# A written-out order of instructions in place of a planner, in a one-core hybrid SSM and attention block

## The chip, the cores and the metric

The kernel runs on one core of a Trainium2 chip. The time is the device time of one execution in microseconds (us). Five engines of the core take part, each with its own stream of instructions, which it runs in the order in which it finds them: PE (TensorE, the matrix multiplications and the transposes), DVE (VectorE), ACT (ScalarE), POOL (GpSimd) and SP (SyncE, which here only issues DMA transfers). An instruction waits on semaphores for the work of other engines, and everything behind it on its own engine waits with it. Nothing about what is computed changes in this case; only the order on each engine does.

## The reference

One layer of a hybrid block over 2048 positions of width 1024 in float32:

```python
hn = rmsnorm(h, mix_norm_g[i])
proj = hn @ w_in[i]
u, g_ssm, q, k, v, g_attn = jnp.split(proj, SPLITS, axis=-1)      # 512 columns each
y_ssm = s5_branch(u, ...) * jax.nn.silu(g_ssm)
y_att = stick_breaking_branch(q, k, v, q_g, k_g) * jax.nn.silu(g_attn)
h = h + jnp.concatenate([y_ssm, y_att], axis=-1) @ w_out[i]
ple_gate = jax.nn.sigmoid(rmsnorm(h, ple_norm_g[i]) @ w_ple_gate[i])
h = h + ple_gate * (p[i] @ w_ple_proj[i])
```

`s5_branch` is a diagonal complex state space model of 32 groups of 16 channels with 64 states each, followed by GELU and a gated linear unit (a 512 x 1024 matrix). `stick_breaking_branch` is causal attention with 8 heads of 64: with z = qk/8, a key's weight is sigmoid(z) times the product of sigmoid(-z) over all later keys before the query, so a block of queries walks through its keys from the latest to the earliest with a running product.

## The kernel before

Positions are handled in 16 tiles of 128. Matrix products of float32 data are made of three passes over a high and a low part of each operand (the three calls at L541 to L543, and L707 to L709). The stages, with the times in the profiled execution:

- **Start** (0 to some 130 us, `phase_u`): x is loaded and normalised (ACT squares and sums at L596, DVE scales the sum, POOL takes the power -1/2 at L507 into `rs_x`, ACT scales x at L598), PE transposes it (`ps_x`, L526), and the first 512 columns of the projection come out as `ps_u` (L541 to L543). The first two tiles are read already transposed (`x_189`, `x_190`, L561); their own sums go over POOL additions (L577) and `rs0`, `rs1` (L581). DVE meanwhile works through a chain of some 300 small operations for the state space tables.
- **State space** (to some 315 us): 8 batches, with the gate's products (`ps_sg`) between them.
- **Attention** (to some 1085 us): 4 pairs of heads, each a pass over the 16 tiles, the passes overlapping. `attn_proj` makes q, k, v and gate of a tile: PE adds up `ps_q` (L745) in two banks, ACT and DVE bring it out (L751, L65), ACT and DVE form the sums of squares (L762, L764, L72), POOL takes the power (`rs_qk`, L507), DVE scales (`qn`, L65), PE transposes (`ps_tq`, L526). v is shifted by one position through two SP transfers (L753, L755) and subtracted on POOL (L756). `attn_block` makes, for each chunk of up to 512 keys, `ps_z` (PE, L812, in two banks, one for each head), `px` (ACT sigmoid L816; POOL mask L819 in the chunk on the diagonal; DVE scan L821), the transposes `ps_wt` (PE, L526), `ws` (two ACT evictions, L835) and `ps_o` (PE, L843).
- **Gated linear unit** (some 860 to 1085 us), among the last attention steps: `ps_v` and `ps_g` (L541 to L543) and their gating on ACT, DVE and POOL (L696, L76, L698), and sums of weight blocks for the last stage (`cross_sums`: SP loads L868, POOL L874 to L877, SP stores L879).
- **Output** (1085 us to the end): `mixed_pair` (products with W_out, `ps_h`) and `gated_pair` (transposes `ps_t`, gate products `ps_g`, `ps_p`, and the stores).

PE works in three modes in this kernel: on all of the array; on halves of the rows (`ps_q`, `ps_z`, `ps_wt`, `ps_tq`: two instructions side by side, `64*128` in the profile); and on halves of the columns (`ps_o`, `128*64`). The transposes `ps_wt` and `ps_tq` all go to one pair of PSUM banks (`e.pair`), so each group of them must wait until the `ws` (or q, k, g) evictions of the group ahead have emptied it. `ps_z` of a chunk must wait in the same way for the scans of the chunk that had its banks.

What sets the order: the program is emitted as one list, tile after tile. Then `plan` works out from addresses which instruction needs which, and `duration` gives each a length by a formula (an SP transfer costs SP 0.45 us whatever it is); `list_schedule` plays the program engine by engine, taking on each the ready instruction of the best rank, with a penalty of 0.09 us for a change of the PE mode and a preference of 4 us for staying in it; `best_order` repeats this forwards and backwards six times and keeps the shortest; `arrange` then ties each instruction to the one ahead of it on its engine. In that model an instruction on PE may start as soon as one that it needs on PE has started, and on the other engines when it is done, with no time in between.

Of the kernel before, what the change touches and what calls it, by code (L numbers as in the profile page):

```python
# [18 lines left out]
P = 128  # L19
# [4 lines left out]
G = 32  # L24
GH = 16
ST = 64
# [1255 lines left out]
def footprint(ap, offset, shape):  # L1282

    row = 1
    for n in shape[1:]:
        row *= n
    p0, m = offset // row, 1
    f = offset % row + sum((n - 1) * s for s, n in ap[1:] if s < 0)
    for s, n in ap[1:]:
        if s and n > 1:  # L1290
            m = sum(m << (abs(s) * k) for k in range(n)) if n * abs(s) > 64 or m != 1 or s not in (1, -1) else (1 << n) - 1
    return p0, p0 + ap[0][1], m << f


def duration(i, name, outs, ins, psum):

    n = max([a[1] for a in outs + ins] or [1])
    eng = str(i.engine).split(".")[-1]
    if name == "InstDMACopy":
        names = [a.bass_ap.tensor.name for a in i.ins if getattr(a, "bass_ap", None) is not None]  # L1300
        return (0.6 if eng == "Pool" else 0.45), (4.0 if any("ssm_w_glu" in k for k in names) else 0.0)
    if name == "InstMatmult":
        cols, kind = outs[0][1], ins[0][2]
        if i.is_transpose:
            return (0.031 if ins[0][0] <= 64 else 0.109), 0.11
        if "float32r" in kind or "bfloat16" in kind:
            return max(cols / 2400.0 + 0.0136, 0.107) / (2 if ins[0][0] <= 64 else 1), 0.11
        half = min(outs[0][0], ins[0][0]) <= 64
        return (0.5 if outs[0][0] <= 32 else 1 if half else 2) * max(cols / 1160.0, 0.056), 0.12
    if eng == "Activation":  # L1310
        return (0.05 if psum else 0.094) + n * 0.00083, 0.065 if psum else 0.03
    if eng == "Pool":
        if name == "InstTensorTensor" and "pow" in str(i.op).lower():
            return 0.35 + 0.15 * n, 0.08
        base, slope = {"InstMemset": (0.04, 0.0008), "InstTensorCopy": (0.4, 0.001), "InstTensorScalarPtr": (0.25, 0.001), "InstTensorScalarAffineSelect": (0.14, 0.0008)}.get(name, (0.12, 0.00186))
        return base + slope * n, 0.09
    if name == "InstTensorScalarPtr" and i.is_tensor_tensor_scan:
        return 0.05 + n * 0.0022, 0.03
    if name in ("InstMemset", "InstTensorCopy", "InstTensorScalarPtr") and not psum and not i_tt(i):
        return 0.07 + n * 0.0006, 0.03  # L1320
    return 0.07 + n * 0.00104, 0.03


def i_tt(i):

    return getattr(i, "is_scalar_tensor_tensor", False)


def plan(tc, pools):

    mybir_i = list(tc.nc.cur_bb.bb.instructions)
    first, last = 16512, 229344
    open_l, open_r, open_b, base, slots, spans, over, home, used = [], [], [], {}, {}, [], {}, {}, {}
    for p in sorted(pools, key=lambda p: p.id):
        kb = int(p.kb_per_partition_size() * 1024)
        sp = str(p.space).split(".")[-1]
        if sp == "DRAM":
            base[p.id] = 0
        else:
            side = open_b if sp == "PSUM" else open_r if "right" in str(p.side) else open_l  # L1340
            born = int(p.alloc_inst.name.split("-")[1])
            while side and side[-1][2] is not None and side[-1][2] < born:
                side.pop()
            at = side[-1][0] if side else 0 if side is open_b else last if side is open_r else first
            lo = at - kb if side is open_r else at
            end = p.release_inst
            side.append((lo if side is open_r else lo + kb, p.id, None if end is None else int(end.name.split("-")[1])))
            base[p.id] = lo
            for q, l2, h2, e2, s2 in spans:
                if sp == s2 and l2 < lo + kb and lo < h2 and e2 is not None and int(e2.name.split("-")[1]) < int(p.alloc_inst.name.split("-")[1]):  # L1350
                    over.setdefault(p.alloc_inst.name, []).append(e2.name)
            spans.append((p.id, lo, lo + kb, end, sp))
        for sp, size, tag, addr, _ in p.gen_slots(0):
            home[tag] = p.alloc_inst.name, p.release_inst.name if p.release_inst is not None else None
            slots.setdefault(tag, []).append((str(sp).split(".")[-1], base[p.id] + addr, size // P))
    turn, tiles, held, pre, length, opened, soft, mode = {}, {}, {}, [], [], {}, [], {}
    number = {i.name: k for k, i in enumerate(mybir_i)}
    for k, i in enumerate(mybir_i):
        if type(i).__name__ == "BassTilePoolBoundary":
# [5 lines left out]
        for w, accs in ((0, i.ins), (1, i.outs)):  # L1365
            for a in accs:
                b = getattr(a, "bass_ap", None)
                if b is None:
                    continue
                t, n = b.tensor, 1  # L1370
                ap = [(int(s), int(c)) for s, c in b.ap]
                for s, c in a.ap[1:]:
                    n *= int(c)
# [249 lines left out]
```

## Time and profile before

| | |
|---|---|
| median of 3 runs | 1476.32 us (1475.82 to 1478.0) |
| profiled execution | 1474.24 us, of which the profile's span is 1472.5 us |
| mean granted TensorE clock | 0.994 |
| PE busy | 1436.7 us (98%) |
| DVE, ACT, POOL busy | 1009.0 (69%), 810.4 (55%), 474.8 us (32%) |
| DMA | 238.21 MB, 162 GB/s on average |

The span is the time between the first and the last record of the engines. The busy time of PE is that in which at least one matrix instruction is under way; weight loads (PEld) run beside it. PE's idle time is therefore 1472.5 - 1436.7 = 35.8 us, and the time that PE spends on changes of mode, or at a lower clock, is part of its busy time.

### The profile page before, as it was taken

The numbers are of one execution on the slowest core, as the hardware profiler recorded it, in microseconds if no ns is written. First come the engines' busy times: TensorE is split into PE (matmuls) and PEld (weight loads), VectorE is DVE, ScalarE is ACT, GpSimd is POOL, SyncE is SP. The second block draws the span as 40 slices with busy tenths as digits, with TensorE's granted clock in tenths as the row PEclk, the third lists the DMA queues.
The fourth block names the chain that finished last, engine by engine and source line by source line (L and its number), as shares of the span: only waits on it lengthen the run. The fifth ranks groups of instructions, "written<-read, shape, count | busy, mean of one in ns | idle before, by whom it ended". The sixth has DMA issues, their size and how long they took to land.

```text
span 1472.5 us, 33586 instructions
## 1 busy us (share of the span) xinstructions
PE 1436.7 (98%) x13068; PEld 1224.2 (83%) x13068; DVE 1009.0 (69%) x1817; ACT 810.4 (55%) x1765; POOL 474.8 (32%) x512
## 2 busy tenths in 40 slices
PE   6999999999999999999999999999999999999998
PEld 5999889988888888888888877777778888778786
DVE  8953977977567786678766775666778557754444
ACT  5654555565555766567655665555665345533432
POOL 3131363522221211221121124443334554534432
PEclk8999999999999999999999999999999999999999
DMA  8886845645333433334332455766568556523221
GB/s 289 288 287 205 250 143 186 206 143 168 128 130 125 144 112 114 114 130 140 121 126 102 142 146 171 226 218 178 155 201 280 176 171 200 166 65 101 93 72 58
DMA packets 179054, 238.21 MB, mean 162 GB/s; under 512 B 65760, under 2 KB 121296, under 8 KB 167760
## 3 DMA queue, kind: packets, MB, share of 16 engines
q1 hardware_dynamic: 176512, 227.49, 48.0%
q0 software_dynamic: 2384, 8.59, 2.0%
q8 instruction: 103, 1.69, 0.5%
q14 instruction: 55, 0.45, 0.1%
HBM read 166.94 MB, written 64.90 MB: 157 GB/s over the span
## 4 chain that ended last, share of the span: by engine, by line
PE 81%; DVE 7%; DMA 3%; ACT 3%; issue 3%; POOL 2%; SPq 1%; POOLq 0%; DVEq 0%; ACTq 0%
PE ps_q L745 21%; PE ps_o L843 7%; PE ps_z L812 6%; PE ps_wt L526 4%; PE ps_g L707 4%; PE ps_h L709 4%; PE ps_h L707 3%; PE ps_h L708 3%; PE ps_g L709 3%; PE ps_g L708 3%; DMA v<-qn 2%; PE ps_u L541 1%; PE ps_u L543 1%; PE ps_u L542 1%; PE ps_sg L541 1%
## 5 line engine op out<-in xcount | busy, mean ns | idle before, releaser
L821 DVE TENSOR_TENSOR_SCAN px<-px,ps_z 128x512 f32<-128x512 f32 (+3 forms) x320 | 339.9, 1086 | 85.9 <-ACT px L816 61.0
L745 PE MATMUL ps_q<-w_w,xt 64*128 64x512 f32 x2784 | 376.7, 399 | 1.3 <-DVE qn L65 0.7
L745 PEld LDWEIGHTS ps_q<-w_w,xt 64*128 64x128 f32 x2784 | 270.8, 185 | 39.7 <-DVE qn L65 2.2
L816 ACT ACTIVATE px<-ps_z 128x512 f32<-128x512 f32 (+3 forms) x320 | 159.2, 535 | 81.0 <-PE ps_z L812 79.8
L835 ACT ACTIVATE ws<-ps_wt 128x512 f32<-128x512 f32 (+3 forms) x320 | 160.7, 539 | 72.0 <-PE ps_wt L526 67.1
L812 PE MATMUL ps_z<-k,q 64*128 64x512 f32 (+3 forms) x960 | 137.7, 379 | 3.7 <-DVE px L821 1.8
L843 PE MATMUL ps_o<-ws,v 128*64 128x128 f32 x2176 | 134.9, 276 | 0.0
L843 PEld LDWEIGHTS ps_o<-ws,v 128*64 128x64 f32 x2176 | 117.3, 137 | 17.6 <-issue 14.7
L507 POOL TENSOR_TENSOR rs_qk<-rs_qk,mhalf 128x4 f32<-128x4 f32 x64 | 67.7, 1058 | 150.7 <-DVE rs_qk L72 148.1
L526 PEld LDWEIGHTS ps_wt<-ident,px 64*128 64x128 f32 x2176 | 95.5, 138 | 24.3 <-ACT ws L835 5.2
L812 PEld LDWEIGHTS ps_z<-k,q 64*128 64x128 f32 x960 | 87.9, 186 | 21.7 <-issue 5.4
L526 PE MATMUL ps_wt<-ident,px 64*128 64x64 f32 x2176 | 100.7, 224 | 2.0 <-ACT ws L835 1.8
L819 POOL TENSOR_SCALAR_AFFINE_SELECT px<-px 128x128 f32<-128x128 f32 x128 | 40.7, 328 | 164.2 <-ACT px L816 154.3
L756 POOL TENSOR_TENSOR v<-qn,v 128x128 f32<-128x128 f32 x64 | 32.2, 503 | 167.6 <-DMA v<-qn 153.9
L541 PE MATMUL ps_u<-xt,w_w 128*128 128x256 f32 x256 | 76.0, 298 | 7.5 <-ACT w_w L491 6.2
L65 DVE TENSOR_TENSOR yr<-sx,yr 128x512 fp32r<-128x512 f32 x64 | 50.6, 814 | 42.2 <-ACT yr L513 41.8
L543 PE MATMUL ps_u<-xt,w_w 128*128 128x256 f32 x256 | 74.5, 297 | 1.9 <-DVE w_w L76 1.8
L542 PE MATMUL ps_u<-xt,w_w 128*128 128x256 f32 x256 | 75.3, 295 | 0.5 <-DVE xt L65 0.5
L1032 POOL TENSOR_TENSOR sg<-sg,h 128x512 f32<-128x512 f32 x28 | 40.1, 1437 | 92.1 <-DVE sg L65 91.9
L513 ACT ACTIVATE yr<-sx 128x512 fp32r<-128x512 f32 x64 | 39.1, 627 | 53.7 <-POOL sx L912 22.6
L65 DVE TENSOR_TENSOR qn<-ps_q,part 128x512 f32<-128x512 f32 x54 | 36.8, 682 | 42.6 <-ACT part L751 39.0
L513 ACT ACTIVATE yr<-yq 128x512 fp32r<-128x512 f32 x48 | 30.2, 629 | 53.3 <-PE ps_h L709 24.5
(438 smaller groups left out, 3486.5 us busy)
## 6 DMA issues: line engine op xcount, KB each, us to landing
xt<-hn SPq DMA_DIRECT2D x58, 1024.0 KB
hn<-xt SPq DMA_DIRECT2D x16, 1024.0 KB
h<-h SPq DMA_DIRECT2D x64, 256.0 KB
wst<-in_w_in_dram SPq DMA_DIRECT2D x48, 256.0 KB
xg<-hn SPq DMA_DIRECT2D x12, 1024.0 KB
out_dram<-sg SPq DMA_DIRECT2D x31, 256.0 KB
x<-in_x_dram SPq DMA_DIRECT2D x14, 512.0 KB
h<-in_x_dram SPq DMA_DIRECT2D x28, 256.0 KB
```

Of the source, the lines that this page charges most:

```text
L526: e.nc.tensor.transpose(ps[h][:, 64 * k:64 * k + 64], v[r], e.ident[r, r])
L541: mm(out, wh, xh, start=first, stop=False)
L542: mm(out, wh, xl, start=False, stop=False)
L543: mm(out, wl, xh, start=False, stop=last)
L707: mm(out, xh, wh, start=first, stop=False, skip_group_check=more)
L709: mm(out, xl, wh, start=False, stop=last, skip_group_check=more)
L745: nc.tensor.matmul(o, xt[r, a, c], A.w[c][r, b], start=c + s == 0, stop=c == NC8 - 1 and s == 2)
L812: nc.tensor.matmul(z[:, :n], q[half[h], a], A.k[ch][half[h], b, :n], start=s == 0, stop=s == 2)
L816: nc.scalar.activation(px[:, :n], z[:, :n], AF.Sigmoid, scale=-(HD ** -0.5))
L821: nc.vector.tensor_tensor_scan(rv, rv, z[:, :n][:, ::-1], initial=1.0 if carry[h] is None else carry[h], op0=ALU.mult, op1=ALU.bypass)
L835: nc.scalar.activation(dst, ps, AF.Copy, bias=1.0, scale=-1.0)
L843: nc.tensor.matmul(po[half[h], :P], A.v[sb][:, h], w[:, h, b], start=sb == i, stop=sb == 0)
```

## The change

The planner (`footprint`, `duration`, `plan`, `list_schedule`, `best_order` and their helpers) is taken out. In its place stands `_ORDER`, a packed table: for each of the five engines, in the order in which the program emits its instructions, which of those left over comes next. `written_order` unpacks it and `arrange` ties the neighbours together as before.

```diff
-def list_schedule(ops, pre, soft, length, mode, rank, near=4.0, change=0.09):
...
-def best_order(ops, pre, soft, length, mode, rows, turns=6):
...
+_ENGINES = ("PE", "DVE", "Activation", "Pool", "SP")
+_ORDER = (
+    'c-qxmTZ|>gS+1(Scb`k2%UsS}c4ubKnd|QC#k;fK-ElnYb?jYhcfI!RI*z@BfWV58Lr6$06GfH@5JHG@!BLQ6gb_j}5U@gUKtep_0VE!I-~pis'
...
+)
+
+
+def written_order(ops):
+
+    import base64, zlib
+    code = iter(zlib.decompress(base64.b85decode(_ORDER)))
+    for e in _ENGINES:
+        left = [i for i in ops if type(i).__name__ != "BassTilePoolBoundary" and str(i.engine).split(".")[-1] == e]
+        line = []
+        while left:
+            at, shift, c = 0, 0, 128
+            while c & 128:
+                c = next(code)
+                at |= (c & 127) << shift
+                shift += 7
+            line.append(left.pop(at))
+        yield line
 
 
 def arrange(tc, pools, rows):
-    ops, pre, *rest = plan(tc, pools)
-    _, order, _ = best_order(ops, pre, *rest, rows)
     info = mybir.DependencyInfo(mybir.DependencyClass.NoSync, mybir.DependencyReason.DATA)
-    for line in order.values():
+    for line in written_order(list(tc.nc.cur_bb.bb.instructions)):
         for a, b in zip(line, line[1:]):
-            tc.add_manual_dep(ops[b], ops[a].name, info, reason="arrange")
+            tc.add_manual_dep(b, a.name, info, reason="arrange")
```

Each engine has the same instructions in both programs (11720 matrix instructions on PE). Up to L1280 the line numbers are the same. The order differs on every engine. Three places follow; a number behind a name tells one tile from another, and is the same in both programs.

The first place is POOL at the start of the program. `x_189` and `x_190` are the two tiles that come in transposed, `rs_x_289` and `rs_x_321` the norms of the third and fourth tile. Before:

```order
L577 TENSOR_TENSOR x_189<-x_189 128x512
L577 TENSOR_TENSOR x_189<-x_189 128x256
L577 TENSOR_TENSOR x_189<-x_189 128x128
L577 TENSOR_TENSOR x_190<-x_190 128x512
L581 TENSOR_TENSOR rs0_148<-rs0_148,mhalf_146 128x1
L577 TENSOR_TENSOR x_190<-x_190 128x256
L507 TENSOR_TENSOR rs_x_289<-rs_x_289,mhalf_146 128x1
L577 TENSOR_TENSOR x_190<-x_190 128x128
L581 TENSOR_TENSOR rs1_149<-rs1_149,mhalf_146 128x1
L507 TENSOR_TENSOR rs_x_321<-rs_x_321,mhalf_146 128x1
```

And with the change:

```order
L577 TENSOR_TENSOR x_189<-x_189 128x512
L577 TENSOR_TENSOR x_189<-x_189 128x256
L577 TENSOR_TENSOR x_189<-x_189 128x128
L507 TENSOR_TENSOR rs_x_289<-rs_x_289,mhalf_146 128x1
L577 TENSOR_TENSOR x_190<-x_190 128x512
L581 TENSOR_TENSOR rs0_148<-rs0_148,mhalf_146 128x1
L577 TENSOR_TENSOR x_190<-x_190 128x256
L507 TENSOR_TENSOR rs_x_321<-rs_x_321,mhalf_146 128x1
L577 TENSOR_TENSOR x_190<-x_190 128x128
L581 TENSOR_TENSOR rs1_149<-rs1_149,mhalf_146 128x1
```

`rs_x_289` now stands ahead of three operations that it stood behind, `rs_x_321` ahead of two. On ACT the sums at L596 that feed them move ahead of the scaling of `x_190` (L575) in the same way, and on PE the products with the diagonal matrices (L585) move behind the transposes of the third and fourth tile, with the transposes of the fifth after them, ahead of the next `ps_u`.

The second place is POOL near the end of the gated linear unit, around the power for the last tile but one of the attention projections (`rs_qk_16155`). Before:

```order
L756 TENSOR_TENSOR v_15532<-qn_15799,v_15532 128x128
L874 TENSOR_TENSOR old_16914<-old_16914 128x512
L875 TENSOR_TENSOR old_16914<-old_16915,old_16914 128x512
L876 TENSOR_TENSOR old_16915<-old_16915,old_16914 128x512
L756 TENSOR_TENSOR v_15800<-qn_16090,v_15800 128x128
L507 TENSOR_TENSOR rs_qk_16155<-rs_qk_16155,mhalf_146 128x4
L877 TENSOR_TENSOR old_16915<-old_16915 128x512
L698 TENSOR_TENSOR old_16190<-old_16190 128x512
L819 AFFINE_SELECT px_16281<-px_16281 128x128
```

And with the change:

```order
L874 TENSOR_TENSOR old_16914<-old_16914 128x512
L507 TENSOR_TENSOR rs_qk_16155<-rs_qk_16155,mhalf_146 128x4
L875 TENSOR_TENSOR old_16914<-old_16915,old_16914 128x512
L876 TENSOR_TENSOR old_16915<-old_16915,old_16914 128x512
L877 TENSOR_TENSOR old_16915<-old_16915 128x512
L698 TENSOR_TENSOR old_16190<-old_16190 128x512
L756 TENSOR_TENSOR v_15800<-qn_16090,v_15800 128x128
L698 TENSOR_TENSOR old_16222<-old_16222 128x512
L819 AFFINE_SELECT px_16281<-px_16281 128x128
```

The power moves ahead of two of the four sums and of the subtraction for v, which waits for a transfer; the mask of `px_16281` now stands behind two gating products (L698) where it stood behind one.

The third place is PE in the attention, around the transposes `ps_wt_5640` and the next ones. Here the rows carry no numbers, and x16 is a run of 16 instructions of a kind. Before, from the group `ps_wt_5684` on:

```order
L526 MATMUL ps_wt<-ident,px 128x64 x16
L745 MATMUL ps_q<-w_w,xt 128x512 x18
L526 MATMUL ps_wt<-ident,px 128x64 x4
L745 MATMUL ps_q<-w_w,xt 128x512 x18
L526 MATMUL ps_tq<-ident,qn 128x64 x4
L526 MATMUL ps_tq<-ident,gn 128x64 x2
L812 MATMUL ps_z<-k,q 128x512 x6
L843 MATMUL ps_o<-ws,v 64x128 x18
```

And with the change, from the group `ps_wt_5640` on, the next group being `ps_wt_5684`:

```order
L526 MATMUL ps_wt<-ident,px 128x64 x16
L812 MATMUL ps_z<-k,q 128x512 x6
L745 MATMUL ps_q<-w_w,xt 128x512 x6
L526 MATMUL ps_wt<-ident,px 128x64 x16
L843 MATMUL ps_o<-ws,v 64x128 x10
L812 MATMUL ps_z<-k,q 128x512 x6
L745 MATMUL ps_q<-w_w,xt 128x512 x24
L812 MATMUL ps_z<-k,q 128x256 x6
L526 MATMUL ps_wt<-ident,px 128x64 x4
```

Between two groups of transposes there were 18 half-row products and are now 12, and the 18 products `ps_o`, one run before, are cut into 10 and 8 (the 8 come further down, behind the next `ps_q`).

Over the whole program the two orders count like this. Changes of the PE mode: 238 before and 252 with the change (between halves of rows and halves of columns 130 and 156, between halves of rows and the whole array 76 and 72, between the whole array and halves of columns 16 and 8, the rest alike). Places where a full group of 16 `ps_wt` is followed by the next group on the same banks after no more PE work than 12 half-row products take (1.36 us at the pace of the trace): 2 before and 27 with the change. Places where the banks of a full chunk's `ps_z` are used again after less than 2.9 us of PE work, at the same pace: 35 before and 19 with the change.

More of the change, by code (lines that the diff above doesn't have):

```diff
@@ L1279, in hybrid_block_kernel @@
     wstack.close()
[L1282 to L1321, printed above, removed]
```

275 lines of the change are left out of this document (66 added, 209 removed).

## The prediction

> **What bounds the kernel now.** I read the page first, for the shares and the chain that ended last:
>
> ```profile
> PE 1436.7 (98%) x13068; PEld 1224.2 (83%) x13068; DVE 1009.0 (69%) x1817; ACT 810.4 (55%) x1765; POOL 474.8 (32%) x512
> PE 81%; DVE 7%; DMA 3%; ACT 3%; issue 3%; POOL 2%; SPq 1%; POOLq 0%; DVEq 0%; ACTq 0%
> ```
>
> PE is the bound nearly everywhere. An order cannot take away a matrix instruction, so it can act on three things only: the 1472.5 - 1436.7 = 35.8 us in which PE idles, the cost of changing from one kind of work to another, which is hidden in PE's busy time, and the clock. The table of windows by stage (columns: the window, its length, then busy time of PE, PEld, DVE, ACT, POOL, the granted clock, the DMA share, GB/s) tells where the idle time lies:
>
> ```profile
> 0.00:37.00 37.00, 23.44 (x147) 21.01 (x148) 32.21 (x165) 21.05 (x36) 14.07 (x27) 0.85 0.82 289
> 37.00:300.00 263.00, 259.90 (x2208) 246.90 (x2208) 198.31 (x430) 143.24 (x305) 94.69 (x62) 1.00 0.69 221
> 300.00:340.00 40.00, 36.95 (x369) 32.72 (x370) 30.50 (x64) 25.21 (x59) 7.74 (x17) 1.00 0.48 157
> 340.00:860.00 520.00, 516.94 (x6445) 442.16 (x6441) 370.21 (x645) 319.81 (x782) 104.41 (x195) 1.00 0.40 128
> 860.00:1085.00 225.00, 220.09 (x2061) 173.93 (x2063) 143.29 (x193) 127.67 (x260) 87.00 (x89) 0.99 0.60 180
> 1250.00:1472.50 222.50, 214.89 (x989) 172.44 (x988) 118.45 (x160) 89.57 (x151) 85.11 (x61) 1.00 0.29 94
> ```
>
> Length less PE's busy time: 13.6 us in the start, 3.1 before 300 us, 3.0 at the entry to the attention, 3.1 in the 520 us of pure attention, 4.9 beside the gated linear unit, 7.6 in the output (the window left out, 1085 to 1250, has the missing 0.5). Then PE's own list of waits (what waited, for whom: sum, times, longest):
>
> ```profile
> PE ps_u L541 <- ACT w_w L491: 6.2, 1, 6.2
> PE ps_g L707 <- ACT yr L513: 2.8, 6, 1.2
> PE ps_tq L526 <- DVE qn L65: 2.2, 2, 1.3
> PE ps_wt L526 <- ACT ws L835: 1.8, 4, 0.6
> PE ps_z L812 <- DVE px L821: 1.8, 2, 1.6
> PE ps_u L543 <- DVE w_w L76: 1.8, 2, 1.5
> PE ps_x L526 <- ACT x L598: 1.8, 2, 1.4
> ```
>
> There is no one large wait; each of these is a place where the order asked for something a little too early.
>
> **The change part by part.**
>
> *Start.* Six of the 13.6 us are the first wait for data. In the new SP order the load of the first weights stands one issue earlier; the first issue stands 0.44 us ahead of the second (the first two rows below), so I count 0.4 us. The rest hangs on the norms of the third and fourth tile (timeline rows: start, duration, and in brackets the idle time ahead and who ended it):
>
> ```profile
> 0.74 0.38 SPq L1102 DMA_DIRECT2D gmix<-in_small_dram  x1
> 1.18 0.89 SPq L561 DMA_DIRECT2D x<-in_xt_dram  x2
> 20.62 4.71 POOL L577 TENSOR_TENSOR x<-x 128x512 f32<-128x512 f32 x4 [14.25 <-ACT x L575]
> 26.53 0.55 POOL L507 TENSOR_TENSOR rs_x<-rs_x,mhalf 128x1 f32<-128x1 f32 x1
> 27.12 1.15 ACT L598 ACTIVATE x<-x,rs_x 128x1024 f32<-128x1024 f32 x1 [2.18 <-POOL rs_x L507]
> 31.43 1.11 PE L526 MATMUL ps_x<-ident,x 64*128 64x64 f32 x16 [1.40 <-ACT x L598]
> 33.72 0.58 PE L541 MATMUL ps_u<-xt,w_w 128*128 128x256 f32 x1 [1.17 <-ACT xt L513]
> ```
>
> ACT idled 2.18 us for `rs_x`, which on POOL stood behind additions and a power for the other tiles. The new order puts it ahead of them, and ACT's sums for it one L575 (about 1 us) earlier, so the scaling can begin up to 2.2 us earlier, after which ACT's own queue is the limit. Part of this is used up: the transposes of the fifth tile now stand ahead of `ps_u` and need one scaling more before PE goes on. I take -2.5 us for the start, and as bounds -5 (all of it, and a shorter spell at the low clock, below) and +0.5 (the fifth tile is as late as all that was won).
>
> *Gated linear unit.* Here the largest stalls outside the start lie:
>
> ```profile
> 957.22 1.01 POOL L507 TENSOR_TENSOR rs_qk<-rs_qk,mhalf 128x4 f32<-128x4 f32 x1
> 958.90 0.34 PE L526 MATMUL ps_tq<-ident,qn 64*128 64x64 f32 x4 [1.29 <-DVE qn L65]
> 1016.43 0.46 POOL L756 TENSOR_TENSOR v<-qn,v 128x128 f32<-128x128 f32 x1 [2.79 <-DMA v<-qn]
> 1016.85 1.01 POOL L507 TENSOR_TENSOR rs_qk<-rs_qk,mhalf 128x4 f32<-128x4 f32 x1
> 1019.53 0.34 PE L526 MATMUL ps_tq<-ident,qn 64*128 64x64 f32 x4 [0.87 <-DVE qn L65]
> 1021.54 1.85 PE L812 MATMUL ps_z<-k,q 64*128 64x512 f32 x6 [1.60 <-DVE px L821]
> 1022.00:1024.00 2.00, 1.91 (x8) 1.09 (x8) 0.55 (x3) 0.94 (x3) 0.00 (x0) 0.64 1.01 358
> 1024.00:1026.00 2.00, 2.00 (x6) 1.56 (x5) 1.36 (x3) 1.79 (x4) 0.29 (x1) 0.50 0.46 166
> 1026.00:1028.00 2.00, 2.00 (x26) 1.43 (x26) 1.79 (x2) 0.00 (x0) 2.00 (x2) 1.00 0.40 141
> ```
>
> At 1016 us POOL waited 2.79 us for the transfer of v, and the power behind it, and so `qn`, the transposes and the mask of the next chunk, were late: 0.87 and 1.60 us of PE. The two together cost more than their length: in the next two windows the clock was 0.64 and 0.50, that is 2.00 x 0.36 + 2.00 x 0.50 = 1.7 us of full-clock work lost. In the new order the power stands ahead of that wait and of two sums. The power of 957.22 us keeps its place behind its sums, but the work on PE between the tile's last `ps_q` and its `ps_tq` grows, added up by the steady pace of each kind, from 7.8 to 14.6 us (at 1019 us from 12.5 to 23.4). The mask at L819 now stands behind two gating products, but the gated work that these wait for is also ahead of that chunk's `ps_z` on PE. All together 1.29 + 0.87 + 1.60 + 1.7 = 5.5 us; I take -4.7, since some of it should return where the mask is late, with the bounds -6.5 (the smaller stalls of the 4.9 us too) and 0.
>
> [...]
>
> *Attention.* The 35 places at which full chunks used their `ps_z` banks again after less than 2.9 us of PE work become 19, and `ps_tq` stands further behind its `ps_q` throughout. At most the 3.1 us idle time of 340 to 860 us can go; I take -1. At the entry (300 to 340 us) the two stalls keep their causes: 0.
>
> *Output.* Of the 2.8 us that `ps_g` waits for `yr`, the longest wait is 1.2 and the other five make 1.6. The order puts some 0.5 us more work between the transposes and the first product that needs them in two of the eight pairs of tiles. With the long wait partly covered I take -0.7 of the 2.8 us; bounds -2.8 and 0.
>
> *What it costs: modes.* 14 more changes of the PE mode (252 for 238). The first price comes from one visit to the half-row mode, the second from the list of PEld's waits:
>
> ```profile
> 1013.57 0.39 PE L541 MATMUL ps_g<-zr,w_w 128*128 128x512 f32 x1
> 1013.89 0.62 PE L812 MATMUL ps_z<-k,q 64*128 64x256 f32 x6
> 1016.21 0.39 PE L541 MATMUL ps_g<-zr,w_w 128*128 128x512 f32 x1
> 1016.44 0.39 PE L542 MATMUL ps_g<-zr,w_w 128*128 128x512 f32 x1
> PEld ps_o L843 <- issue: 14.7, 42, 0.4
> ```
>
> Undisturbed, one full product follows the other by 0.23 us; into the other mode it took 0.32, so 0.1 us more. At `ps_o`, where most of the new changes are, the weight load stood 14.7 / 42 = 0.35 us at the issue. I take 0.2, nearer to the first since a load runs partly beside PE: 14 x 0.2 = +2.8 us, bounds 14 x 0.1 = +1.4 and 14 x 0.35 = +4.9.
>
> *What it costs: the pair of banks for transposes.*
>
> ```profile
> L835 ACT ACTIVATE ws<-ps_wt 128x512 f32<-128x512 f32 (+3 forms) x320 | 160.7, 539 | 72.0 <-PE ps_wt L526 67.1
> 398.97 2.32 PE L745 MATMUL ps_q<-w_w,xt 64*128 64x512 f32 x18
> 396.15 0.71 PE L526 MATMUL ps_wt<-ident,px 64*128 64x64 f32 x16 [0.64 <-ACT ws L835]
> ```
>
> Eighteen half-row products took 2.32 us with the tail of the last, so about 0.114 us each; 12 are 1.36 us. The two `ws` evictions that must end in this time are 2 x 0.539 = 1.08 us when ACT is free. What is left, 0.28 us, has to hold the way from PE to ACT and back, and anything that ACT is still doing. Behind these 12 products wait the next transposes and all of PE. At 396.15 us such a place cost 0.64 us; the four in the list cost 1.8 / 4 = 0.45. There are 25 more with the change. Free ACT: 0; one other ACT operation of 0.54 us in the way each time: 25 x 0.54 = +13.5 us. ACT is busy 55% of the time, but at a place laid out for it mostly not; I take +1.5 us (0.06 each).
>
> *Sum.* -2.5 - 4.7 - 1 - 0.7 + 2.8 + 1.5 = -4.6 us. Against the profiled execution (1474.24, its span 1472.5 and 1.74 around it) that is 1469.6; the median of the runs lies 2.1 us above the profiled one, so I put the median at 1476.32 - 4.6 = 1471.7 us.
>
> **The rivals.** What a measurement of this kernel can tell from no change is about 0.2%, 2.95 us.
>
> *The stalls only move.* PE is 98% busy, and each stall comes from a chain through three or four engines; the next link may be as late as the one moved. For it: after the wait at L756 the mask, the scan and the banks stand next. Against it: the distance on PE nearly doubles there. Without the gated unit's gain the sum is +0.1: 1476.4 us.
>
> *The tight pair of banks decides (slower).* If ACT is late by one operation at most of the 25 places, +12.4 us in place of +1.5, the sum is -4.6 + 10.9 = +6.3: 1482.6 us. It decides from (6.1 + 2.95) / 25 = 0.36 us a place, the gains less the modes being 8.9 - 2.8 = 6.1. For it: in 18 of the 27 places the ACT instruction just ahead of the evictions is a `px` sigmoid. Against it: that sigmoid's `ps_z` was finished some 2 us earlier in most of them.
>
> *More comes back.* Waits below what shows as idle time (the `ps_z` banks, 16 places fewer) and the low clock of the start go too: -5 - 6.5 - 2.5 - 2 + 1.4 + 0 = -14.6: 1461.7 us.
>
> That the change does not do what it says can be left out: the rows of both programs show another order on every engine.
>
> **How the numbers follow.** The forecast 0.46, nothing measurable 0.20, slower 0.20, more 0.14. The forecast's own range is 1467 to 1476. For 8 times in 10 I go to 1458 (the large gain and a little) and 1484 (the tight banks). Faster by over 0.2% (below 1473.4): most of the forecast (0.39) and the large gain (0.14) make 0.53. Within 0.2%: 0.07 + 0.18 = 0.25. Slower: 0.22.
>
> **What would show it.** Right: the first `ps_u` of the third tile begins before 33.7 us; the waits of `ps_tq` for `qn` and of `ps_z` for `px` in 860 to 1085 us are gone and no window there has a clock under 0.9; over the span PE's idle time falls by some 8 us while its busy time grows by some 3. Wrong: a sum of waits of `ps_wt` for `ws` above 6 us, or a new cluster of stalls over 2 us with a low clock behind it, or stalls at the mask behind two L698.

## The result, and the profile after

The kernel with the written-out order takes 1461.09 us in the median of four runs (1459.94 to 1463.52), the kernel before 1476.47 us beside it. The ratio is 0.9897 with an interval of 0.9879 to 0.9914, a gain of 15.4 us. The forecast was 1471.7 us; the time lies inside the range (1458 to 1484), next to the case "more comes back" (1461.7). The direction was right and the size was not: a gain of 4.6 us was forecast.

The page of the changed kernel, busy time and chain:

```profile
PE 1426.1 (98%) x13068; PEld 1217.2 (83%) x13068; DVE 1013.0 (69%) x1817; ACT 809.7 (55%) x1765; POOL 463.0 (32%) x512
PE 83%; DVE 5%; DMA 4%; issue 4%; POOL 2%; ACT 2%; SPq 0%; POOLq 0%; DVEq 0%; ACTq 0%
```

The span is 1459.3 us for 1472.5, so 13.2 us less. (The other 2.2 us of the 15.4 are that the profiled execution of before lies 2.2 us under its median, and that of the change on it.) PE idles for 1459.3 - 1426.1 = 33.2 us, where it was 35.8. So only 2.6 us of the gain are idle time that went. The other 10.6 us went out of PE's **busy** time, although PE does the same matrix instructions. That is the reverse of the forecast, by which idle time falls by some 8 us and busy time grows by some 3, and it is what had to be explained.

The windows by stage (the same columns as before; the stages end a little earlier, so the limits differ):

```profile
0.00:37.00 37.00, 24.26 (x170) 21.77 (x171) 31.98 (x165) 24.50 (x41) 13.68 (x27) 0.87 0.85 300
300.00:340.00 40.00, 35.98 (x344) 31.45 (x344) 28.11 (x52) 23.48 (x55) 7.73 (x17) 0.96 0.49 157
340.00:860.00 520.00, 519.68 (x6513) 442.83 (x6510) 382.18 (x660) 322.03 (x791) 102.44 (x196) 1.00 0.40 129
860.00:1075.00 215.00, 213.05 (x2097) 172.19 (x2097) 141.99 (x186) 128.98 (x262) 86.62 (x91) 0.99 0.62 191
1075.00:1240.00 165.00, 161.86 (x774) 132.09 (x771) 110.88 (x163) 80.05 (x167) 77.81 (x60) 1.00 0.64 208
1240.00:1459.30 219.30, 211.27 (x973) 169.27 (x971) 116.37 (x154) 87.63 (x146) 83.56 (x61) 1.00 0.28 92
```

In the attention PE idles 0.3 us where it idled 3.1, beside the gated unit 2.0 where it idled 4.9; at the entry (300 to 340 us) it idles 4.0 for 3.0, and in the output (the last two rows) 11.2 for 8.1. In the 520 us of attention the trace has 6513 rows of matrix instructions for 6445. PE's list of waits (what waited, for whom: sum, times, longest):

```profile
PE ps_u L541 <- ACT w_w L491: 6.1, 1, 6.1
PE ps_g L707 <- ACT yr L513: 3.5, 4, 2.2
PE ps_h L709 <- DVE yr L65: 2.4, 2, 1.8
...
PE ps_z L812 <- DVE sg L65: 1.8, 1, 1.8
PE ps_g L541 <- ACT old L696: 1.8, 1, 1.8
...
PE ps_z L812 <- DVE px L821: 0.8, 1, 0.8
...
PE ps_wt L526 <- ACT g L791: 0.3, 1, 0.3
```

The waits of `ps_tq` for `qn`, and beside the gated unit those of `ps_z` for `px`, are gone from the list, as forecast (the 0.8 us left for `px` lie at 334.06 us, at the entry). Gone too are those of `ps_wt` for `ws`, where the forecast had put a cost. New are one at the entry (`ps_z` for `sg`), one at the start of the gated unit (`ps_g` for `old`), and two in the output (`ps_h` for `yr`).

To see where the time went, I compare the moments at which both executions had done the same amount of matrix work, each instruction counted at the steady pace of its kind. The change is ahead by 2.3 us at the end of the start, by 2.9 at 277 us, by 0.5 when the attention is fully under way (366 us), by 8.7 at its end (848 us of before), by 16.5 at the end of the gated unit (1077.7 us of before), and by 13.1 at the end. So: start -2.3, entry +2.4, attention -8.2, gated unit -7.8, output +3.4.

### The profile page after: what moved, and what is told of

It reads as the page before. It is cut to its first block, busy times and chain, and to the rows that moved or that the text cites. A ratio compares the mean times of both kernels' runs of the same rounds, so it can differ in the third digit from the quotient of the medians.

```text
span 1459.3 us, 33550 instructions
## 1 busy us (share of the span) xinstructions
PE 1426.1 (98%) x13068; PEld 1217.2 (83%) x13068; DVE 1013.0 (69%) x1817; ACT 809.7 (55%) x1765; POOL 463.0 (32%) x512
## 4 chain that ended last, share of the span: by engine, by line
PE 83%; DVE 5%; DMA 4%; issue 4%; POOL 2%; ACT 2%; SPq 0%; POOLq 0%; DVEq 0%; ACTq 0%
PE ps_q L745 23%; PE ps_o L843 8%; PE ps_z L812 7%; PE ps_wt L526 5%; PE ps_g L707 4%; PE ps_g L709 3%; PE ps_g L708 3%; PE ps_h L709 3%; PE ps_h L707 3%; PE ps_h L708 3%; PE ps_sg L541 1%; PE ps_sg L543 1%; PE ps_sg L542 1%; DMA tb<-tabs 1%; PE ps_v L541 1%
## 5 line engine op out<-in xcount | busy, mean ns | idle before, releaser
L745 PE MATMUL ps_q<-w_w,xt 64*128 64x512 f32 x2784 | 364.5, 397 | 0.0
L745 PEld LDWEIGHTS ps_q<-w_w,xt 64*128 64x128 f32 x2784 | 265.2, 186 | 43.8 <-issue 1.9
L835 ACT ACTIVATE ws<-ps_wt 128x512 f32<-128x512 f32 (+3 forms) x320 | 156.3, 538 | 85.0 <-PE ps_wt L526 81.7
L812 PE MATMUL ps_z<-k,q 64*128 64x512 f32 (+3 forms) x960 | 132.7, 376 | 2.7 <-DVE sg L65 1.8
L526 PEld LDWEIGHTS ps_wt<-ident,px 64*128 64x128 f32 x2176 | 90.2, 139 | 24.6 <-ACT ws L835 6.5
L526 PE MATMUL ps_wt<-ident,px 64*128 64x64 f32 x2176 | 97.7, 224 | 0.4 <-ACT g L791 0.3
L541 PE MATMUL ps_u<-xt,w_w 128*128 128x256 f32 x256 | 66.9, 293 | 7.0 <-ACT w_w L491 6.1
L542 PE MATMUL ps_u<-xt,w_w 128*128 128x256 f32 x256 | 66.5, 291 | 1.1 <-DVE xt L65 1.1
L543 PE MATMUL ps_u<-xt,w_w 128*128 128x256 f32 x256 | 65.1, 294 | 1.5 <-DVE w_w L76 1.5
```

Of the source, the lines that this page charges most:

```text
L526: e.nc.tensor.transpose(ps[h][:, 64 * k:64 * k + 64], v[r], e.ident[r, r])
L541: mm(out, wh, xh, start=first, stop=False)
L745: nc.tensor.matmul(o, xt[r, a, c], A.w[c][r, b], start=c + s == 0, stop=c == NC8 - 1 and s == 2)
L812: nc.tensor.matmul(z[:, :n], q[half[h], a], A.k[ch][half[h], b, :n], start=s == 0, stop=s == 2)
L835: nc.scalar.activation(dst, ps, AF.Copy, bias=1.0, scale=-1.0)
```

## The experiments

In this part "up to 320" and the like are us of matrix work done on PE, counted as above. The orders of before and of the change for one stretch can be put together, on all five engines, because both programs have the same instructions.

**One stretch at a time.** Three kernels take the change's order in one stretch only, one takes it everywhere but in the output.

The attention alone:

```diff
-order: BEFORE
+order: BEFORE up to 320, CHANGE up to 760, BEFORE from there
```

> The order of before everywhere, save for the stretch of pure attention (a third to four sevenths of PE's work, about 366 to 848 us in the trace of before), which has the order of the change. In the two traces the same PE work took 8.2 us less in this stretch. If the gain belongs to this stretch's own order, the time is 1476.4 - 8 = about 1468 us (1467 to 1470). Rival: the gain there was handed on from what the stages ahead left in flight; then at most half of it remains, 1472 us or more.

Measured: 1469.19 us (1467.51 to 1470.89, five runs) beside 1475.8, ratio 0.9958 (0.9945 to 0.9971): -6.6 us. The attention's part of the gain is there when nothing else is changed.

The gated unit alone:

```diff
-order: BEFORE
+order: BEFORE up to 760, CHANGE up to 958, BEFORE from there
```

> The order of before, save for the stretch with the gated linear unit (848 to 1077 us in the trace of before), which has the order of the change. In the traces the change took 7.8 us less there. If this gain belongs to the stretch: 1475.8 - 7.8 = 1468 us (1467 to 1470). Rival: without the attention's order ahead of it less is in hand, 1472.

Measured: 1468.6 us (1467.76 to 1469.63, five runs) beside 1476.35, ratio 0.9948 (0.9934 to 0.9962): -7.75 us.

The start alone:

```diff
-order: BEFORE
+order: CHANGE up to 60, BEFORE from there
```

> The order of the change for the first 60 us of PE's work, then that of before. In the traces the change is 2.3 us ahead after the start, which my sum had put at 2.5: 1475.8 - 2.3 = 1473.5 us. Rival: the lead is used up where the state space part waits for its tables and transfers: 1475.5 us.

Measured: 1475.0 us (1471.48 to 1477.9, twelve runs), ratio 0.999 (0.998 to 1.0001). The median is 1.35 us lower, between the 2.3 us that were expected and the 0.3 us of the rival, and the interval just reaches 1. So the times do not show the start's gain, and do not decide against the rival; it rests on the profiles.

Everything but the output:

```diff
-order: CHANGE
+order: CHANGE up to 958, BEFORE from there
```

> The order of the change up to the start of the output stage (five sevenths of PE's work), and the order of before from there on. The traces say that the change loses 3.4 us in the output stage, by new waits of ps_h for yr (1.8 and 0.6 us) and a longer one of ps_g for yr (2.2 us for 1.2). If that loss belongs to the output's own order: 1461.1 - 3.4 = about 1457.7 us. Rival: the earlier stages ran ahead and the data for the output (weights over DMA) would be late whatever the order; then 1461 us.

Measured: 1458.51 us (1455.75 to 1459.66, four runs), ratio to before 0.9887 (0.9872 to 0.9903). That is the lowest time of all kernels of the block here, 2.6 us under the change, and 1.9 us when each is taken against the kernel before that ran beside it. The intervals of the two ratios overlap, so against the change the times alone do not settle it. All that PE waits for in the output in this kernel's list of waits:

```profile
PE ps_g L707 <- ACT yr L513: 2.9, 6, 1.2
```

The waits of `ps_h` that the change has there are gone, and those of `ps_g` are back at what before had (2.8 in six). The largest `ps_h` wait of the change, in its timeline (start, duration, in brackets the idle time ahead and who ended it):

```profile
1091.66 3.47 DVE L65 TENSOR_TENSOR w_wc<-wst,w_wc 128x512 fp32r<-128x512 f32 x2
1095.05 0.68 DVE L65 TENSOR_TENSOR yr<-yq,yr 128x512 fp32r<-128x512 f32 x1
1095.78 0.51 PE L709 MATMUL ps_h<-w_w,yr 128*128 128x512 f32 x1 [1.81 <-DVE yr L65]
```

Two preparations of weights stand ahead of `yr` on DVE and take 3.47 us, and PE is at the product that needs `yr` 1.81 us too early. (Before has two such preparations ahead of a `yr` as well, and no wait behind them; what differs is the work that PE still has ahead of the product.)

**One cause inside the gated unit.** On POOL alone, in before: the power `rs_qk` of the tile whose `ps_tq` waited at 958.9 us goes ahead of four sums, and the power of the tile at 1019.5 us ahead of two sums and the subtraction for v.

```diff
+L507 TENSOR_TENSOR rs_qk<-rs_qk,mhalf 128x4
 L874 TENSOR_TENSOR old<-old 128x512
 L875 TENSOR_TENSOR old<-old 128x512
 L876 TENSOR_TENSOR old<-old 128x512
 L877 TENSOR_TENSOR old<-old 128x512
-L507 TENSOR_TENSOR rs_qk<-rs_qk,mhalf 128x4
...
 L874 TENSOR_TENSOR old<-old 128x512
+L507 TENSOR_TENSOR rs_qk<-rs_qk,mhalf 128x4
 L875 TENSOR_TENSOR old<-old 128x512
 L876 TENSOR_TENSOR old<-old 128x512
 L756 TENSOR_TENSOR v<-qn,v 128x128
-L507 TENSOR_TENSOR rs_qk<-rs_qk,mhalf 128x4
```

> The order of before with one edit on POOL: the power rs_qk_15335 ahead of the four sums it stood behind, and rs_qk_16155 ahead of two sums and of the subtraction for v. From the trace of before: the sums of squares are ready at 952.7 and 1010.8 us, the powers ran at 957.2 and 1016.9. If POOL's order is what made these stalls: ps_tq no longer waits (1.29 + 0.87 us), ps_z at 1021.5 still waits 1.4 us for the mask: -2.4 us, and -4 if the spell at the low clock goes too: 1472 to 1473.5. Rival (the gain of this stage came from the work that PE has ready meanwhile): the chain finds a next late link, 1475 to 1476.

Measured: 1474.08 us (twelve runs) beside 1476.35 (23 runs), ratio 0.9981 (0.997 to 0.9993): -2.3 us. In its trace:

```profile
1013.67 1.01 POOL L507 TENSOR_TENSOR rs_qk<-rs_qk,mhalf 128x4 f32<-128x4 f32 x1 [3.38 <-DVE rs_qk L72]
1021.40 0.34 PE L526 MATMUL ps_tq<-ident,qn 64*128 64x64 f32 x4
1022.93 1.54 PE L812 MATMUL ps_z<-k,q 64*128 64x512 f32 x6 [1.13 <-DVE px L821]
```

The windows behind:

```profile
1022.00:1024.00 2.00, 0.99 (x5) 0.63 (x6) 1.45 (x3) 0.12 (x1) 0.40 (x2) 1.00 0.90 247
1024.00:1026.00 2.00, 2.00 (x12) 1.27 (x8) 1.03 (x1) 1.66 (x4) 0.00 (x0) 1.00 1.00 322
```

The power ran at 1013.67 in place of 1016.85, the transposes at 1021.40 no longer wait, and the clock behind them stays at 1.00. Of the 1.60 us of `ps_z` behind them 1.13 remain: the mask and the scan of that chunk are the next link. So the powers were the cause of the two `ps_tq` stalls. The 2.3 us are close to the 2.4 that were expected without a gain in clock, and about a third of what the change gains in this stage.

**Kinds of work on PE: is it the changes of mode?** The forecast charged 0.2 us for each of 14 more changes. Two kernels move `ps_o` to another neighbour. First the change, in 41 places, with six `ps_q` between the transposes and `ps_o`:

```diff
 L526 MATMUL ps_wt<-ident,px 128x64 x16
+L745 MATMUL ps_q<-w_w,xt 128x512 x6
 L843 MATMUL ps_o<-ws,v 64x128 x10
 L812 MATMUL ps_z<-k,q 128x512 x6
-L745 MATMUL ps_q<-w_w,xt 128x512 x24
+L745 MATMUL ps_q<-w_w,xt 128x512 x18
```

> The order of the change with one edit on PE: at 41 places where a run of ps_o followed on transposes (ps_wt, ps_tq), six ps_q that came a little later are put between. The number of mode changes stays 252. Theory D (a change of mode waits until the last instruction ahead of it has drained, so its price depends on what that is: 0.323 us from the start of a ps_q to that of a ps_o, 0.152 from a transpose, at a steady pace of 0.113 and 0.030, so 0.21 and 0.12 lost): 41 x 0.09 = 3.7 us slower, and up to 2 more for the 41 added changes of kind: 1464.8 to 1467. Rival W (the attention gains by waits for ACT and DVE alone): ps_o comes later behind its ws, nothing lost, 1461 us or a little less.

Measured: 1518.05 us, ratio to before 1.029 (1.0275 to 1.0304): +57 us on the change, where the one side expected 4 to 6 and the other none. Two rows of its list of waits, with 16.2 of the 57 us, show the kind of wait that came in:

```profile
PE ps_q L745 <- DVE qn L65: 11.3, 25, 1.3
...
PE ps_q L745 <- ACT part L751: 4.9, 15, 0.6
```

The six products often opened a new group of `ps_q`, and PE waited there for the engines that still read its bank. So the run says nothing on modes. The second kernel, in before, moves 33 runs of `ps_o` behind the next transposes:

```diff
 L812 MATMUL ps_z<-k,q 128x512 x6
 L745 MATMUL ps_q<-w_w,xt 128x512 x6
+L526 MATMUL ps_wt<-ident,px 128x64 x8
 L843 MATMUL ps_o<-ws,v 64x128 x10
-L526 MATMUL ps_wt<-ident,px 128x64 x8
 L745 MATMUL ps_q<-w_w,xt 128x512 x12
```

> The order of before with one edit on PE: at 33 places where a run of ps_o followed on ps_q or ps_z, it is moved behind the next transposes (ps_wt, ps_tq). The number of runs of a kind and of mode changes stays as it was. Theory D: 33 x 0.09 = 3.0 us faster, 1473.4 us. Rival W: 1476.4 us, or slower where the later ps_o holds up yat or the ws buffers.

Measured: 1509.79 us, ratio 1.0234 (1.0218 to 1.0249): +34 us, where a small gain was expected. Its waits:

```profile
PE ps_wt L526 <- ACT ws L835: 9.9, 12, 3.3
...
PE ps_z L812 <- DVE px L821: 6.4, 10, 1.1
PE ps_tq L526 <- DVE qn L65: 5.4, 5, 1.5
```

What both show is how much hangs on the distances: 33 to 41 runs moved past one neighbour, by about 1 us of PE work each, cost 34 to 57 us. For the price of a mode, PE had to be taken by itself. First in short rounds, each repeated 20 times:

```diff
-the block
+for seq in (((q, 12), (wt, 16)), ((q, 12), (z, 6)), ((q, 12), (wt, 16), (o, 8)), ((wt, 16), (q, 12), (o, 8)), ((q, 12), (o, 8))):
+    for _ in range(20):
+        for f, n in seq:
+            f(n)
```

> Not the block: one kernel that copies x's first tile to the output and lets PE run on fixed operands, six series of 20 rounds (after 240 ps_q-like products at a steady pace): 12 q + 16 wt; 12 q + 6 z; 12 q + 16 wt + 8 o; 16 wt + 12 q + 8 o; 12 q + 8 o (q and z: half-row products of 512 columns; wt: half-row transposes of 64; o: half-column products of 128). No other engine is waited for. Theory D: the third and fourth series hold the same instructions and the same number of changes of mode, and differ by about 0.09 us a round in favour of the third, where the change into o follows on transposes; a change of kind inside the half-row mode (q to wt and back) costs 0.05 us or less for both ways together. Rival: a change of mode costs the same whatever is ahead, the two series differ by less than 0.03 us a round. A third: a change of kind inside a mode costs 0.1 us or more; then the 80 fewer of the attention would explain its gain by themselves.

Measured in one execution. Two rounds of the first series, by the transposes (L44 of that kernel):

```profile
66.53 0.65 PE L44 MATMUL b<-ident,raw 64*128 64x64 f32 x15
68.46 0.65 PE L44 MATMUL b<-ident,raw 64*128 64x64 f32 x15
```

From one to the next it is 1.93 us, while 12 half-row products and 16 transposes at their steady pace are 12 x 0.1134 + 16 x 0.030 = 1.84: going into the transposes and back costs 0.09 us. In the same way, `ps_q` to `ps_z` and back costs nothing measurable (2.04 us for 18 x 0.1134 = 2.04), one visit to `ps_o` from `ps_q` and back 0.39 us. The rounds of three, transposes - `ps_q` - `ps_o` and `ps_q` - transposes - `ps_o`, take 3.116 and 3.120 us: the neighbour of `ps_o` made no difference to the round, so what is saved on the way into it is paid at another change. Theory D asked for 0.09 us between the two; found are 0.004, the other way.

Then PE alone runs the whole attention, in the order of before and in that of the change, with no other engine to wait for:

```diff
-the block
+run("q", 512, 240)
+for text in (BEFORE, CHANGE):
+    for r in text.split():
+        k, n = r[1:].split("x")
+        run(r[0], int(k), int(n))
+    run("q", 512, 240)
```

> Not the block: PE alone runs, on fixed operands and with no other engine to wait for, the 5240 matrix instructions that the stretch of pure attention has in both orders, kinds and widths as they stand there: first in the order of before (475 runs of a kind), then in that of the change (462), each followed by 240 products at a steady pace. In the kernel the stretch took 581.8 - 8.2 us less with the change. Priced by the series measured alone (0.093 us for a visit to the transposes from the projections, 0.385 for a visit to ps_o, 0.033 for transposes that touch ps_o, none between ps_q and ps_z) the change should be shorter by 2 us (1 to 3.5). Then the other 6 us are waits for ACT and DVE, most of them too short to show as idle time. Rival 1: the replay itself is shorter by 6 us or more, the gain is in the grouping of kinds. Rival 2, as my prediction had it: it is longer, by up to 3 us, for its 7 more visits to ps_o.

Measured in one execution; the two pieces as windows (the granted clock, third from the end, is 1.00 in both; each `ps_o` instruction shows as two rows, so the 5240 instructions are some 5955 rows):

```profile
34.05:502.95 468.90, 468.90 (x5957) 396.83 (x5954) 0.00 (x0) 0.00 (x0) 1.00 0.01 2
530.15:999.15 469.00, 469.00 (x5958) 401.36 (x5955) 0.00 (x0) 0.00 (x0) 1.00 0.01 2
```

468.90 and 469.00 us: the change's order is no shorter, and the expected 2 us are refuted. The changes of kind cost some 31 us in each (at the steady pace both would be some 437.5), and they come out the same, although the kinds follow each other differently: the change goes from transposes straight into `ps_o` 44 times for 17, and from `ps_q` to transposes 83 times for 99.

With this, the two profiles can be read anew. Over the part of the piece that can be laid record on record, before takes 466.31 us (371.1 to 837.4) for what PE alone does in 456.56: **9.75 us of waiting, of which 2.6 show as PE's idle time**. The change takes 459.10 us (376.3 to 835.4) for 457.28: 1.82 us, of which 0.3 show. The kernel with the attention's order alone (1.67) and the one with before's output (1.67) repeat this for the change's order, those with the unit or the start alone (10.65 and 10.49) for before's.

The same for the gated unit and the output:

```diff
-for text in (BEFORE, CHANGE):
+for text in (UNIT_BEFORE, UNIT_CHANGE, OUTPUT_BEFORE, OUTPUT_CHANGE):
```

> Not the block: PE alone, without waits for other engines, runs the 1821 matrix instructions that both programs have in the gated unit's stretch, first in the order of before and then of the change, and then the 1870 of the output in both orders, with 240 half-row products between the four pieces. In the attention the same trial gave 468.9 us for the order of before and 469.0 for that of the change, so that all of the gain there was time spent waiting. Theory (waits here too): the gated unit's two orders within 1 us of each other alone, although the change gained 7.8 us there; the output's two orders within 1 us, although the change lost 3.4 us there. Rival (the output's loss is PE's own): the change cuts the output's work into 252 runs of one kind for 123, and its order alone is longer by 2.5 to 4 us. Rival (the unit's gain is PE's own, by fewer changes of mode): its order alone is shorter by 2 us or more.

Measured in one execution, the four pieces:

```profile
35.26:246.20 210.94, 210.94 (x2077) 168.84 (x2074) 0.00 (x0) 0.00 (x0) 1.00 0.01 1
273.55:483.29 209.74, 209.74 (x2078) 169.31 (x2074) 0.00 (x0) 0.00 (x0) 1.00 0.01 1
510.73:896.43 385.70, 385.70 (x1950) 318.78 (x1948) 0.00 (x0) 0.00 (x0) 1.00 0.00 1
923.88:1310.11 386.23, 386.23 (x1952) 318.22 (x1950) 0.00 (x0) 0.00 (x0) 1.00 0.00 1
```

The unit's order of the change is 1.2 us shorter on PE alone (a little more than the 1 us that the first theory allowed, less than the 2 of its rival), the output's 0.5 longer, far from the 2.5 to 4 of the rival. The rest is waiting:

| stretch | PE's own time, change - before | lost above PE alone, before | the same, change | of it idle on PE, before and change |
|---|---|---|---|---|
| attention | +0.1 | 9.75 | 1.82 | 2.6, 0.3 |
| gated unit | -1.2 | 10.96 | 4.61 | 5.4, 2.0 |
| output | +0.5 | 8.23 | 10.95 | 3.4, 6.7 |

(us; a stretch of the low clock counts as lost.) Waiting -7.9, -6.4 and +2.7, PE's own time -0.6 in all, and the 0.5 us by which the change was ahead at 366 us: together -12.7 of the 13.2 us between the spans.

**What a wait looks like that does not show.** One of the larger ones in before, the first two rows from PE, the third from PEld:

```profile
586.24 0.98 PE L812 MATMUL ps_z<-k,q 64*128 64x256 f32 x6
587.16 0.46 PE L526 MATMUL ps_wt<-ident,px 64*128 64x64 f32 x8
...
586.60 0.41 PEld L812 LDWEIGHTS ps_z<-k,q 64*128 64x128 f32 x5 [0.18 <-DVE px L821]
```

The second of six products waits for the scan of the chunk that had its bank. PE's row shows no idle time, because the first product's bar still runs; but the row is 0.98 us long, where the same six took 0.62 at 1013.89 us (in the prediction). The 0.36 us are counted as busy. The first bar is 0.381 us long; the second product starts 0.366 us behind the first, where at 1013.89 us it followed by 0.003, so the bar covers all of the wait. Only the row of PEld names it. Laid on PE alone, cut at the changes of kind, 39 pieces of the attention of before lose more than 0.03 us, 9.6 us in all, and 15 pieces with 1.6 us in the change. (With PE alone, whatever else the other engines might do to PE while they work is missing too. A slowing of that sort would be spread over all of some 470 pieces; here nearly all of the loss sits in 39, so it is called waiting.)

## Why the prediction was right, and where it was not

**Start**, -2.5 forecast, -2.3 found in the profiles (the times of the kernel with the start alone do not show it). The mechanism held:

```profile
23.56 0.58 POOL L507 TENSOR_TENSOR rs_x<-rs_x,mhalf 128x1 f32<-128x1 f32 x1 [1.75 <-DVE rs_x L72]
24.17 1.15 ACT L598 ACTIVATE x<-x,rs_x 128x1024 f32<-128x1024 f32 x1 [2.00 <-POOL rs_x L507]
33.17 0.58 PE L541 MATMUL ps_u<-xt,w_w 128*128 128x256 f32 x1
```

ACT scales the third tile at 24.17 for 27.12, and the first `ps_u` of that tile begins at 33.17 for 33.72, before the 33.7 that was set as the sign.

**Gated linear unit**, -4.7 forecast, -6.4 of waiting found (and -1.2 on PE itself, which belongs to the modes). The term was right in kind and too small: moving the powers takes out the two `ps_tq` stalls (-2.3 us by itself), the `ps_z` wait goes too, which the powers alone do not bring, and waits that do not show as idle were left out of the sum. (10.96 - 5.4 less the 1.7 us of low clock leaves 3.9 us of them in before; 4.61 - 2.0 less the like leaves some 1 us in the change.) One sign failed: a new stall at the start of the stage was followed by a low clock once more (below), so a window under 0.9 is still there, in another place. And the 1.7 us of low clock that the sum counted as a gain were not sure. The kernels with the attention's order alone and with the start's alone keep before's order here and have the same stall of 1.60 us (at 1017.32 and 1020.13 us, behind one of 0.4 us, where before has 0.87), and the clock behind it stays at 1.00 in both; in the first of them it falls behind another stall, of 2.46 us at 953.78.

**Attention**, -1 forecast, -7.9 found (the tight pair of banks included). This is the step that failed most: "At most the 3.1 us idle time of 340 to 860 us can go". The time that could go was 9.75 us, since three quarters of the waiting lay inside the bars of PE. The case "more comes back" had named waits below what shows as idle time, the `ps_z` banks among them, but gave them little (the terms of its sum carry no names; 2 or 2.5 us is the most that can be meant). They were 7.2 in the attention of before (9.75 - 2.6) and 1.5 in the change's. That these waits went is what the table shows. Sorted by the instruction at which the delay against PE alone begins in the trace, before loses 4.1 us at transposes, 3.9 at `ps_q` and 1.5 at `ps_z`, the change 1.2, 0.3 and 0.1. So the `ps_z` banks, which the prediction named, were the smallest part. No run changes one of these distances by itself, so which of them brought how much stays a reading of the traces.

**Modes**, +2.8 forecast, -0.6 found for the three stretches on PE alone. The price of 0.2 us a change was near for a visit from `ps_q` to `ps_o` and back (0.39 us for two changes). The step that failed is to multiply the number of changes by it: a change has no price of its own here, it depends on the two kinds at it (0.09 us for the transposes from `ps_q` and back, nothing for `ps_z`, 0.39 for `ps_o`), and what is saved at one change is paid at another of the same round (3.116 and 3.120 us). The upper price of 0.35 us came from PEld's idle time at the issue, which is idle time of the weight loads and not of PE. It stands in the same way in the list of the kernel in which PE runs the attention alone (here too between 371 and 837 us):

```profile
PEld b L112 <- issue: 4.6, 13, 0.4
PEld b L110 <- issue: 4.3, 25, 0.2
```

**The pair of banks for transposes**, +1.5 forecast. The pairs of transposes that stand close do show, in PEld's waits between 371 and 837 us, of before and then of the change:

```profile
PEld ps_wt L526 <- ACT ws L835: 2.6, 4, 0.9
```

```profile
PEld ps_wt L526 <- ACT ws L835: 4.9, 28, 0.3
```

28 waits in place of 4, but none over 0.3 us, where four had 2.6 us with one of 0.9. Since the change loses 1.82 us above PE alone in this whole stretch, the 28 together cost at most that. All that begins at transposes there is 1.2 us, where it was 4.1 before, so this term had even the wrong sign. The rival that this pair decides is refuted: its 0.36 us a place would have been 9 us.

**Output**, -0.7 forecast, +2.7 found. The step that failed looked at two of the eight pairs of tiles and at the wait that was there, and took the other products to be safe. Four waits up to 2.2 us took the place of six up to 1.2, and `ps_h` waits came in that were not there before.

**Entry**, 0 forecast, +2.4 found. The stall of 1.57 us there moved to another instruction and became 1.82, with a low clock behind it in this profile: 1.7 of the 2.4 us, which by the last section the same stall did not cost in another kernel.

The sum was too small by 13.2 - 4.6 = 8.6 us of span. In what was found less what was forecast: attention with its pair of banks -7.9 - (-1 + 1.5) = -8.4, modes -3.4, gated unit -1.7, output +3.4, entry +2.4; the rest is under 1 us. The range held the time because the case "more comes back" was in it, with the right reason at a third of its size or less, and because two errors went the other way. That the time lies within 1 us of that case is luck: its start (-5) brought 2.3 us, and the output, for which it has no loss, lost 2.7 us.

## What to carry to other kernels

Idle time of the bounding engine is a lower bound of its waiting, not the most that a better order can bring: 2.6 us of idle time stood for 9.75 of waiting in the attention here, because `ps_q` has bars of 0.399 us that at a steady pace start every 0.1134, so that a wait of up to nearly 0.3 us is counted as busy. Run the bounding engine's own sequence alone, once in each order; what the kernel takes above that is the waiting, and what the two sequences differ in is the price of the order itself. And move a run of work only with its distances in view, to the bank that it fills and the operand that it needs: one neighbour too far cost 34 to 57 us here, ten times what the prices of the moved work promised.

## What the runs showed of the hardware that was not expected

**The clock dropped behind one stall and not behind its like.** Three stalls of nearly one length in the change are that at 1095.78 us (1.81, above) and these two:

```profile
312.78 0.55 PE L812 MATMUL ps_z<-k,q 64*128 64x128 f32 x6 [1.82 <-DVE sg L65]
...
872.99 0.50 PE L541 MATMUL ps_g<-zr,w_w 128*128 128x512 f32 x1 [1.76 <-ACT old L696]
```

The windows behind the three:

```profile
314.00:316.00 2.00, 2.00 (x12) 1.85 (x10) 0.73 (x2) 0.00 (x0) 0.38 (x2) 0.52 0.92 278
316.00:318.00 2.00, 2.00 (x16) 1.86 (x15) 0.00 (x0) 0.27 (x1) 0.00 (x0) 0.62 0.45 133
874.00:876.00 2.00, 2.00 (x24) 1.74 (x22) 1.53 (x2) 1.54 (x4) 1.21 (x3) 0.50 0.13 45
...
1096.00:1098.00 2.00, 2.00 (x10) 1.61 (x10) 2.00 (x4) 1.64 (x4) 0.00 (x0) 1.00 0.88 301
```

The kernel with before's output, whose order is the same at the first of them, has that stall too, at 313.00 us and again 1.82 us long. The window behind it there:

```profile
314.00:316.00 2.00, 2.00 (x22) 1.95 (x19) 0.94 (x3) 0.09 (x1) 0.60 (x2) 1.00 0.92 290
```

So the stall of 1.82 us was followed by a clock of 0.52 and 0.62 in one execution, and by 1.00 in the other. After 1.81 us (1095.78) it stayed at 1.00, and so it did after the longest of the later stalls, 2.23 us at 1246.28; after 1.76 us (872.99) it fell to 0.50. Where it falls, 2.00 x 0.48 + 2.00 x 0.38 = 1.7 us are lost. A stall of this length carried a risk of 1.7 us in these rows, not a price, and such a drop is likely to be part of what separates one execution of a kernel from another (the run of the change with 1463.52 us has a mean clock of 0.991, that with 1459.94 us one of 0.995). What decides whether it falls, the runs do not show.

**A change of kind cost as a round, not as an event.** Half-row products and transposes are one mode (`64*128` in the profile), yet going between them and back cost 0.09 us; `ps_q` and `ps_z` cost nothing (2.04 us measured, 2.04 at the steady pace). A visit to `ps_o`, another mode (`128*64`), cost 0.39 us from `ps_q` and back, but the rounds of three kinds are the same in either order (3.116 and 3.120 us). This is so although the way into `ps_o` alone differs: between 371 and 837 us of before the first `ps_o` starts 0.324 us behind the start of a `ps_q` (median of 15), and 0.152 behind that of a transpose `ps_wt` (median of 12). Both are 0.07 us before the end of the bar ahead, as at all 90 changes between these two modes there (0.068 to 0.071; the profile models the ends of the bars).
